# Row-wise dot products and softmax: a 64 KB row pitch in HBM for the halves, and the y loads issued by ScalarE

## The chip, the cores and the metric

The kernel runs on one core of one Trainium2 chip. The metric is device time in microseconds (us) of one launch; before the change it is 327.01 us, the median of three runs (326.87 to 327.13).

## The reference

```
gram = np.matmul(x, y.transpose(0, 2, 1))      # x, y: [8, 4096, 512] float32
diag = np.diagonal(gram, axis1=1, axis2=2)     # [8, 4096]
diag = diag - diag.max(axis=-1, keepdims=True)
exp  = np.exp(diag)
out  = exp / exp.sum(axis=-1, keepdims=True)   # [8, 4096] float32
```

Only the diagonal of the product is used, so the work is 8 x 4096 dot products of length 512, one per row, and a softmax over the 4096 results of each batch. The inputs are 64 MiB each; the output is 128 KiB.

## The kernel before

A batch has 4096 rows, which are spread over 128 partitions, 32 rows to each. The kernel handles a batch in two halves. A half is one "tile": 16 rows per partition of x in an SBUF buffer `xt` (128 partitions x 32 KB, 4 MB) and the same of y in `yt`. There are 16 tiles, numbered 0 to 15 here (batch b has tiles 2b and 2b+1); x7 is the x load of tile 7, y7 its y load. In HBM a half is one stretch of 2048 rows, and partition p takes 16 consecutive rows of it, so that a 4 MB load reads one contiguous 4 MB stretch, 32 KB after 32 KB.

Each pool of buffers has three slots (`bufs=3`). The load of tile n therefore waits until the dot products of tile n-3 are done. All loads are issued by SyncE (SP in the profile) in the order x0, y0, x1, y1 and so on (lines 43 and 44). The last tile is loaded in pieces of 8, 4, 2, 1 and 1 rows per partition, each an x and a y load; they are called a to e here (x15a is 2 MB, x15e is 256 KB). Completion is signalled over eight semaphore lanes that all DMAs use in turn, so a DMA may also wait for the completion of the DMA that had its lane before it.

VectorE (DVE) computes 16 dot products per tile and partition, one instruction for each row (line 51): it multiplies a row of `xt` with a row of `yt` and accumulates the sum into one column of `diag`. After the second half of a batch comes the softmax: a maximum over 32 columns (line 65), a maximum over the partitions on GpSimd (POOL, line 67), its negative (line 69), the exponential with a row sum on ScalarE (ACT, line 71), the sum over the partitions on GpSimd (line 76), a reciprocal and a multiplication on DVE (lines 78 and 79), and the store of the batch's results, 16 KB, issued by ACT (line 80). The store of batch b is called OUTb. Before the change it writes two runs of 64 B per partition.

Every engine executes its instructions in the order of the program as the framework has laid it out, and waits at the first one whose inputs are missing. A DMA issued by SP goes to SP's queue, one issued by ACT to ACT's queue; both queues are served by the same 16 DMA engines. A 4 MB load is 128 packets of 32 KB, 8 on each of the 16 engines.

Of the kernel before, what the change touches and what calls it, by code (L numbers as in the profile page):

```python
# [1 line left out]

# [5 lines left out]


@with_exitstack
def kernel(
    ctx: ExitStack,
    tc: tile.TileContext,
    x: bass.AP,
    y: bass.AP,
    out: bass.AP,
):
    nc = tc.nc
    f32 = mybir.dt.float32  # L20
    B, N, D = x.shape
    P = nc.NUM_PARTITIONS
    R = N // P
    H = R // 2


    xv = x.rearrange("b (h p r) d -> b h p r d", p=P, r=H)
    yv = y.rearrange("b (h p r) d -> b h p r d", p=P, r=H)
    ov = out.rearrange("b (h p r) -> b p h r", p=P, r=H)

    io = ctx.enter_context(tc.tile_pool(name="io", bufs=3))
    persist = ctx.enter_context(tc.tile_pool(name="persist", bufs=1))
    sm = ctx.enter_context(tc.tile_pool(name="sm", bufs=2))

    diag = persist.tile([P, B * R], f32, name="diag")
    res = persist.tile([P, B * R], f32, name="res")

    def load(b, r0, parts):
        xt = io.tile([P, H, D], f32, tag="xt", name="xt")
        yt = io.tile([P, H, D], f32, tag="yt", name="yt")  # L40
        o = 0
        for n in parts:
            nc.sync.dma_start(out=xt[:, o : o + n, :], in_=xv[b, r0 // H, :, o : o + n, :])  # L43
            nc.sync.dma_start(out=yt[:, o : o + n, :], in_=yv[b, r0 // H, :, o : o + n, :])
            o += n
        return xt, yt

    def dots(b, r0, xt, yt):
        for k in range(H):
            c = b * R + r0 + k  # L50
            nc.vector.scalar_tensor_tensor(  # L51
                out=xt[:, k, :],
                in0=xt[:, k, :],
                scalar=1.0,
                in1=yt[:, k, :],
                op0=mybir.AluOpType.mult,
                op1=mybir.AluOpType.mult,
                accum_out=diag[:, c : c + 1],
            )

    def softmax(b):
        db = diag[:, b * R : (b + 1) * R]
        rb = res[:, b * R : (b + 1) * R]
        mxp = sm.tile([P, 1], f32, tag="mxp", name="mxp")
        nc.vector.tensor_reduce(out=mxp, in_=db, axis=mybir.AxisListType.X, op=mybir.AluOpType.max)  # L65
        mx = sm.tile([P, 1], f32, tag="mx", name="mx")
        nc.gpsimd.partition_all_reduce(out_ap=mx, in_ap=mxp, channels=P, reduce_op=bass_isa.ReduceOp.max)  # L67
        nmx = sm.tile([P, 1], f32, tag="nmx", name="nmx")
        nc.vector.tensor_single_scalar(out=nmx, in_=mx, scalar=-1.0, op=mybir.AluOpType.mult)  # L69
        sump = sm.tile([P, 1], f32, tag="sump", name="sump")  # L70
        nc.scalar.activation(  # L71
            out=rb, in_=db, func=mybir.ActivationFunctionType.Exp,
            bias=nmx, scale=1.0, accum_out=sump,
        )
        ssum = sm.tile([P, 1], f32, tag="ssum", name="ssum")
        nc.gpsimd.partition_all_reduce(out_ap=ssum, in_ap=sump, channels=P, reduce_op=bass_isa.ReduceOp.add)  # L76
        rc = sm.tile([P, 1], f32, tag="rc", name="rc")
        nc.vector.reciprocal(out=rc, in_=ssum)  # L78
        nc.vector.tensor_single_scalar(out=rb, in_=rb, scalar=rc, op=mybir.AluOpType.mult)  # L79
        nc.scalar.dma_start(out=ov[b], in_=rb.rearrange("p (h r) -> p h r", r=H))  # L80

    for b in range(B):
        for h in range(2):
            last = b == B - 1 and h == 1
            parts = [8, 4, 2, 1, 1] if last else [H]
            xt, yt = load(b, h * H, parts)
            dots(b, h * H, xt, yt)
        softmax(b)


# [1 line left out]
_INS = ['x', 'y']  # L92
_OUTS = [((8, 4096), 'float32')]


# [23 lines left out]
```

## Time and profile before

| What | Value |
|---|---|
| median of 3 runs | 327.01 us |
| profiled execution, its own time | 327.13 us |
| its span in the profile | 325.4 us |
| DVE busy | 164.4 us (51%) |
| ACT busy, POOL busy | 4.6 us, 6.1 us |
| load queue (q1) | 5760 packets, 134.22 MB, 96.1% of 16 engines' span |
| store queue (q10) | 2176 packets, 0.13 MB, 0.5% |
| mean rate over the span | 413 GB/s |

Times within the profile are counted from the start of the span. The difference of 1.7 us between the profiled execution's time and its span lies outside the profile. A queue's share is the time that its packets took, divided by the time of 16 engines over the whole span. The landing time of a DMA counts from its issue to the signal that all of its data is there, so it contains the time that it spent behind earlier transfers of its queue.

### The profile page before, as it was taken

The page shows a single profiled execution, that of the slowest core. Times are in us where ns is not written, and L with a number is a line of the kernel's source. Part 1 is how long each engine was busy: PE and PEld are TensorE (multiplying, and loading weights), DVE is VectorE, ACT ScalarE, POOL GpSimd, SP SyncE. Part 2 cuts the span into 40 slices and gives each one's busy share as a digit, 9 for nine tenths or more (in the row PEclk, how much of TensorE's full clock was granted, in tenths as well). Part 3 has the DMA queues.
Part 4 walks back from the last instruction along what each step waited for, and adds up shares of the span by engine and source line. Part 5 has one row for each costly group of instructions (what it writes and reads, how often), then busy time and mean ns, then how long its engine had stood idle before and what let it go on. Part 6 is the DMA issues. An engine that isn't in the chain of part 4 may idle for free.

```text
span 325.4 us, 727 instructions
## 1 busy us (share of the span) xinstructions
DVE 164.4 (51%) x544; ACT 4.6 (1%) x17; POOL 6.1 (2%) x20
## 2 busy tenths in 40 slices
DVE  0029084390935619165290833909257190662992
ACT  1000000000000000000000000000000000000000
POOL 0000000000000000000000000000000000000000
DMA  8999999999999999999999999999999999999960
GB/s 322 451 411 427 451 440 403 444 452 403 435 451 424 416 451 432 407 448 448 411 431 452 409 432 447 427 415 448 436 419 435 452 405 436 447 423 414 411 250 5
DMA packets 7941, 134.39 MB, mean 413 GB/s; under 512 B 2816, under 2 KB 2816, under 8 KB 3584
## 3 DMA queue, kind: packets, MB, share of 16 engines
q1 hardware_dynamic: 5760, 134.22, 96.1%
q10 hardware_dynamic: 2176, 0.13, 0.5%
q14 instruction: 5, 0.04, 0.0%
HBM read 134.22 MB, written 0.13 MB: 413 GB/s over the span
## 4 chain that ended last, share of the span: by engine, by line
DMA 82%; DVE 16%; issue 1%; SPq 0%; POOLq 0%; POOL 0%; DVEq 0%
DMA yt<-in_y_dram 82%; DVE xt L51 15%; SPq L43 0%; DVE mxp L65 0%; POOLq L114 0%; POOL mx L67 0%; DVE res L79 0%; DVE rc L78 0%; DVEq L51 0%; DVEq L79 0%; POOLq L67 0%
## 5 line engine op out<-in xcount | busy, mean ns | idle before, releaser
L51 DVE SCALAR_TENSOR_TENSOR xt<-xt,yt 128x512 f32<-128x512 f32 x256 | 158.3, 687 | 144.2 <-DMA yt<-in_y_dram 144.2
L51 DVE DVE_READ_ACCUMULATOR xt<-xt,yt 128x1 f32 x256 | 21.1, 82 | 0.0
L67 POOL PARTITION_ALL_REDUCE mx<-mxp x8 | 2.8, 352 | 309.0 <-DVE mxp L65 309.0
L71 ACT ACTIVATE res<-diag,nmx 128x32 f32<-128x32 f32 x8 | 2.6, 321 | 315.4 <-DVE nmx L69 315.4
L78 DVE RECIPROCAL rc<-ssum 128x1 f32<-128x1 f32 x8 | 1.3, 164 | 7.7 <-POOL ssum L76 7.7
L69 DVE TENSOR_SCALAR nmx<-mx 128x1 f32<-128x1 f32 x8 | 1.2, 154 | 4.3 <-POOL mx L67 4.3
L76 POOL PARTITION_ALL_REDUCE ssum<-sump x8 | 3.1, 385 | 5.8 <-ACT res L71 5.8
L79 DVE TENSOR_SCALAR res<-res,rc 128x32 f32<-128x32 f32 x8 | 1.9, 242 | 0.9
L65 DVE TENSOR_REDUCE mxp<-diag 128x1 f32<-128x32 f32 x8 | 1.5, 186 | 0.3
L71 ACT ACTIVATION_READ_ACCUMULATOR res<-diag,nmx 128x1 f32 x8 | 1.5, 186 | 0.0
L71 ACT ACT_TABLE_LOAD x1 | 1.3, 1283 | 0.7 <-PEq L103 0.7
L103 POOL MEMSET const-float32-0.0<- 128x1 f32 x1 | 0.1, 99 | 0.2 <-issue 0.2
L103 POOL MEMSET const-bfloat16-1.0<- 128x1 bf16 x1 | 0.1, 102 | 0.0
L103 POOL MEMSET const-uint8-127<- 128x1 uint8 x1 | 0.1, 102 | 0.0
L103 POOL MEMSET const-float32-1.0<- 128x1 f32 x1 | 0.1, 99 | 0.0
## 6 DMA issues: line engine op xcount, KB each, us to landing
xt<-in_x_dram SPq DMA_DIRECT2D x15, 4096.0 KB, 39.6
yt<-in_y_dram SPq DMA_DIRECT2D x15, 4096.0 KB, 48.9
xt<-in_x_dram SPq DMA_DIRECT2D x1, 2048.0 KB, 34.8
yt<-in_y_dram SPq DMA_DIRECT2D x1, 2048.0 KB, 39.3
xt<-in_x_dram SPq DMA_DIRECT2D x1, 1024.0 KB, 35.8
yt<-in_y_dram SPq DMA_DIRECT2D x1, 1024.0 KB, 37.9
xt<-in_x_dram SPq DMA_DIRECT2D x1, 512.0 KB, 35.5
yt<-in_y_dram SPq DMA_DIRECT2D x1, 512.0 KB, 27.0
```

Source lines behind the costliest of these rows:

```text
L51: nc.vector.scalar_tensor_tensor(out=xt[:, k, :], in0=xt[:, k, :], scalar=1.0, in1=yt[:, k, :], op0=mybir.AluOpType.mult, op1=mybir.AluOpT ...
L65: nc.vector.tensor_reduce(out=mxp, in_=db, axis=mybir.AxisListType.X, op=mybir.AluOpType.max)
L67: nc.gpsimd.partition_all_reduce(out_ap=mx, in_ap=mxp, channels=P, reduce_op=bass_isa.ReduceOp.max)
L69: nc.vector.tensor_single_scalar(out=nmx, in_=mx, scalar=-1.0, op=mybir.AluOpType.mult)
L71: nc.scalar.activation(out=rb, in_=db, func=mybir.ActivationFunctionType.Exp, bias=nmx, scale=1.0, accum_out=sump,)
L76: nc.gpsimd.partition_all_reduce(out_ap=ssum, in_ap=sump, channels=P, reduce_op=bass_isa.ReduceOp.add)
L78: nc.vector.reciprocal(out=rc, in_=ssum)
L79: nc.vector.tensor_single_scalar(out=rb, in_=rb, scalar=rc, op=mybir.AluOpType.mult)
L103: nc = _bacc.Bacc("TRN2", target_bir_lowering=False, num_devices=1)
```

## The change

Three things are different. Partition p now takes 32 consecutive rows of a batch, and a half is 16 of these 32; a 4 MB load reads 128 runs of 32 KB that start 64 KB apart. The y loads are issued by ACT in place of SP. The output of a batch is one run of 128 B per partition in place of two of 64 B. Sizes of the loads, the pieces of the last tile, the number of buffers and all arithmetic stay as they are.

```diff
-    xv = x.rearrange("b (h p r) d -> b h p r d", p=P, r=H)
-    yv = y.rearrange("b (h p r) d -> b h p r d", p=P, r=H)
-    ov = out.rearrange("b (h p r) -> b p h r", p=P, r=H)
+    xv = x.rearrange("b (p r) d -> b p r d", p=P)
+    yv = y.rearrange("b (p r) d -> b p r d", p=P)
+    ov = out.rearrange("b (p r) -> b p r", p=P)
...
-            nc.sync.dma_start(out=xt[:, o : o + n, :], in_=xv[b, r0 // H, :, o : o + n, :])
-            nc.sync.dma_start(out=yt[:, o : o + n, :], in_=yv[b, r0 // H, :, o : o + n, :])
+            nc.sync.dma_start(out=xt[:, o : o + n, :], in_=xv[b, :, r0 + o : r0 + o + n, :])
+            nc.scalar.dma_start(out=yt[:, o : o + n, :], in_=yv[b, :, r0 + o : r0 + o + n, :])
...
-        nc.scalar.dma_start(out=ov[b], in_=rb.rearrange("p (h r) -> p h r", r=H))
+        nc.scalar.dma_start(out=ov[b], in_=rb)
```

The framework orders the instructions of each engine. On SP only the 20 x loads remain, each behind the release of its buffer. On ACT the order becomes y0, y1, y2, and then for each batch b: the exponential of b, y of tile 2b+3, OUTb, y of tile 2b+4. At the end it is: exponential of batch 6, y15a, OUT6, y15b, y15c, y15d, y15e, exponential of batch 7, OUT7. On DVE two rows of tile 2 now stand inside the softmax of batch 0, ahead of lines 78 and 79; the rest of its order is unchanged, and POOL's too. The lanes that gate the pieces become: x15b waits for OUT4, x15c for x13, x15d for y13, x15e for x14, y15b for y14, y15c for x15a, y15d for x15b, y15e for y15a. Before the change, by the times of SP's issues, y15c waited for x14, x15d for y14, y15d for OUT6 and y15e for y15a.

## Prediction

> **What bounds the kernel now.** I read the page's busy slices and queues first, then the chain of waits, then the instruction groups, then a table of busy time by stretches for the end, and the timeline of the last rows.
>
> ```profile
> span 325.4 us, 727 instructions
> ...
> DMA  8999999999999999999999999999999999999960
> ...
> q1 hardware_dynamic: 5760, 134.22, 96.1%
> q10 hardware_dynamic: 2176, 0.13, 0.5%
> ...
> DMA 82%; DVE 16%; issue 1%; SPq 0%; POOLq 0%; POOL 0%; DVEq 0%
> ...
> L51 DVE SCALAR_TENSOR_TENSOR xt<-xt,yt 128x512 f32<-128x512 f32 x256 | 158.3, 687 | 144.2 <-DMA yt<-in_y_dram 144.2
> ```
>
> The loads occupy all 16 engines from the first slice to the last but one; DVE works half of the time and waits 144.2 us for y. 96.1% of 325.4 us is 312.7 us of work on every DMA engine. A tile is 16 packets of 32 KB on each engine (8 of x, 8 of y); SP's issues, which follow the end of a tile's dot products, stand 19.44 us apart:
>
> ```profile
> 111.30 0.33 SPq L43 DMA_DIRECT2D xt<-in_x_dram  x1
> 111.67 0.43 SPq L44 DMA_DIRECT2D yt<-in_y_dram  x1
> 130.74 0.33 SPq L43 DMA_DIRECT2D xt<-in_x_dram  x1
> ```
>
> So a 32 KB packet takes 19.44 / 16 = 1.21 us (the trace's packet records say 1.213; 0.611, 0.309, 0.159 and 0.084 for 16, 8, 4 and 2 KB). Now the end:
>
> ```profile
> 4.00:309.00 305.00, 153.94 (x509) 2.90 (x14) 5.16 (x14) 1.00 1.00 431
> 309.00:314.00 5.00, 5.00 (x17) 0.00 (x0) 0.00 (x0) 1.00 1.02 393
> 314.00:318.00 4.00, 3.99 (x14) 0.00 (x0) 0.00 (x0) 1.00 0.08 32
> ```
>
> The column before the last is the DMA share: 1.00 until 314, then 0.08, which is one engine of 16 working 4 us longer than the others (four instruction fetches of 8 KB during the span went to it, by the packet records). And DVE, idle half of the time before, is full in these last stretches:
>
> ```profile
> 298.72 0.69 DVE L51 SCALAR_TENSOR_TENSOR xt<-xt,yt 128x512 f32<-128x512 f32 x1 [7.16 <-DMA yt<-in_y_dram]
> ...
> 318.58 0.69 DVE L51 SCALAR_TENSOR_TENSOR xt<-xt,yt 128x512 f32<-128x512 f32 x1 [0.57 <-DMA yt<-in_y_dram]
> ```
>
> From the first row of tile 14 to the last of tile 15 it waits once, 0.57 us. The reader is to see that two things limit the end together: the last bytes (318.5), and the arrival of tile 14 plus 32 rows of DVE. What delays tile 14 by more than 0.6 us delays the end, even where the last bytes come no later.
>
> **Edit 1, the addresses.** Packets keep their sizes; their starts in HBM move from 32 KB to 64 KB apart. No row shows 64 KB. The nearest: the pieces of the last tile already read 16 to 2 KB out of each 32 KB, and their packets run at 0.611 us for 16 KB, twice which is 1.222 against 1.213. Skipping addresses costs nothing there, so I take 0. A gain is excluded, since a packet of 1.213 us already differs by only 9 ns from twice the next smaller; the other end is the poorest stretch with queued loads (share 0.97, 410 GB/s in 292 to 309, against 431), +5% or 15 us.
>
> The Trainium skill, "DMA: Bandwidth & Descriptors", section "Latency and other measured facts", warns of row pitches at large powers of two; its smallest is 512 KiB, at 207 GB/s in each direction, and it falls from 2 MiB up. By it 64 KB costs nothing either, but no run here shows that page's cases.
>
> **Edit 2, the output.** OUT falls from 16 to 8 data packets per engine (2176 / 8 / 16 = 17 with the signal, then 9). At 11 ns by the packet records, seven stores beside loads save 7 x 8 x 0.011 = 0.6 us. OUT7 stays a 2.8 us landing.
>
> **Edit 3, y on ACT: issue.** Twenty issues of 0.43 us leave SP for ACT, 8.6 us on an engine busy for 4.6; covered by the y data already queued. What is new is what stands ahead: y5, for example, waits behind the exponential of batch 1, so for the dots of tile 3 and not of tile 2. These end 9.9 us after tile 3 is complete; the softmax head adds 1 us, the time from issue to first packet another 1: y5 arrives 12 us after tile 3. Its cover is y4, 8 packets, which shared with x last 19.4 us: 7 us to spare, cost 0. Where x is dry, y4 alone lasts 9.7 us and 2 us stand open, but then x's next load, released by the same dots, is due first. OUTb and y(2b+4) come with the softmax tail, 2 us later, behind y(2b+3): 0. If that cover were gone, each uncovered us would cost one only if x's queue were empty too. For OUT0 the two rows of tile 2 ahead of lines 78 and 79 mean waiting for tile 2 (near 62 us) with y3 queued: 0 as well. SP loses the in-order wait of y behind x; x is now held by its buffers alone.
>
> **Edit 3: sharing.** This is where the path moves. How two queues share an engine is shown by OUT, on ACT's queue beside the loads on SP's:
>
> ```profile
> out_dram<-res ACTq DMA_DIRECT2D x8, 16.0 KB, 22.0
> ...
> DMA to landing us min/median/max: 2.8/22.0/23.4
> ```
>
> Alone it lands in 2.8 us, beside loads in 22.0: 19.2 us for 17 packets of 11 ns. Each of them waits for about one 32 KB packet; by the packet records the 17 take 17.5 us, 0.85 turns of 1.213. So engines alternate between queues packet by packet, whatever the size. x and y alone would then advance alike, both landing when y lands now. But OUT now stands in y's queue: while its 9 packets pass, x gets 9 x 0.85 = 7.7 extra packets, nearly a whole 4 MB load (8). After OUT0, x leads by about one load, and nothing returns the lead until x's queue is empty for want of a buffer. The next OUT would make it two; three buffers don't allow more (x(n+3) waits for the dots of n), so x runs dry for a while and y takes both turns. In the middle this costs nothing: some queue always has work, total bytes stay on schedule, only tiles arrive unevenly.
>
> At the end it costs. Say the lead is one load when tile 13 is complete: x14 has landed too, x15a and x15b are in SP's queue (released by the dots of tile 12), and ACT's queue holds OUT5 and then y14. y14 needs 7.7 + 9 = 16.7 turns. In these, x passes x15a (9 turns, 8 x 0.611 = 4.9 us) and 7.7 packets of x15b (x 0.309 = 2.4 us). The engine's work up to y14 grows by L = 7.3 us. Bounds of L: 0 without any lead; all of x15, 8 x (0.611 + 0.309 + 0.159 + 2 x 0.084) = 10.0. I take 7.3, since it follows from the one-load lead, between the two.
>
> The sum: tile 14 starts at 298.7 - 0.6 + 7.3 = 305.4. Then 32 rows of 0.613 (starts 0.61 apart; 9.90 for a tile's rows in the chain) are 19.7 without a wait, since y15a to e, the only loads left for the engines, land by 318, ahead of their rows (tile 15 starts at 315.3). The last row ends at 325.1. From there to the end it was 325.4 - 319.3 = 6.1 (softmax, OUT7, closing). Span 331.2; outside it 327.13 - 325.4 = 1.7: 332.9, and 0.1 less for the median (the profiled execution was 327.13, the median is 327.01): 332.8.
>
> A rule that speaks against any effect of this edit: the same page of the Trainium skill, section "Rules for kernel authors", says that spreading DMAs over SP, ACT and GpSimd does not help, as all interleave on the same 16 engines, and saves issue time only. By it the sum would be the unchanged 327 less 0.6; by the OUT row it is 332.8.
>
> **The rivals.** (a) No lead: if y and OUT in one queue don't lose turns to x, or x is held back, tile 14 comes at 298.1 and the last bytes set the end: 327.0 - 0.6 = 326.4, between 326.0 and 327.5. For it: x's lead needs x loads queued, which the buffers limit. Against: the 22.0 us landing. (b) Faster: two queues hide the fixed 9 ns per packet. Per engine 15 x 16 + 10 x 8 = 320 packets make at most 2.9 us, and OUT 0.6: 323.5. It decides only where a 32 KB packet falls under 1.213 and there is no lead, since a lead over 3.5 us eats it. Against: engines at a share of 1.00. (c) The address pitch or the alternation of two streams costs bandwidth: at 5% some 342; it outweighs the lead once 32 KB packets take over 1.213 + 7.3 / 240 = 1.243 us. The 16 KB pieces speak against it. (d) The full lead, L = 10.0: 335.5.
>
> **How the numbers follow.** 0.2% is 0.65 us, about what a measurement tells from no change. Lead and late tile 14 (329 to 336, with (d)): 0.70. (a): 0.13, of which 0.05 falls beyond -0.65. (b): 0.07. (c): 0.10. Slower: 0.70 + 0.10 + 0.01 = 0.81; same 0.07; faster 0.12. The range leaves out (b) and most of (c): 326.4 to 336.5; the likeliest case's own is 329 to 336.
>
> **What would show it.** Packet shares near 1.00 up to 310 (edit 1 at zero); x landings far earlier than y's of the same tile after the first store; the gaps between tiles' first rows uneven, some near 10 us and others over 20, in place of 19.4; the first row of tile 14 near 305, with DVE never waiting after it; the last bytes still near 318. The prediction is wrong if x and y of a tile land together throughout, if tile 14 starts near 298, or if both queues run empty midway (the share falls under 1), which would add to it.

## The result, and the profile after

The changed kernel takes 331.92 us (median of 4 runs, 331.86 to 332.06), the kernel before 326.94 us: a ratio of 1.0154 (95% interval 1.0137 to 1.0172), 5.0 us slower. The prediction said 332.8. The profiled execution took 331.9 us with a span of 330.0.

The page of the changed kernel, with its busy slices, queues, chain and the group of the dot products:

```profile
span 330.0 us, 732 instructions
...
DVE  0029093470920561910878290660388465191995
...
DMA  8999999999999999999999999999999999999900
...
q10 hardware_dynamic: 4032, 67.24, 47.6%
q1 hardware_dynamic: 2880, 67.11, 47.5%
...
DMA 72%; DVE 24%; issue 2%; POOL 1%; ACTq 0%; POOLq 0%; DVEq 0%; ACT 0%
...
L51 DVE SCALAR_TENSOR_TENSOR xt<-xt,yt 128x512 f32<-128x512 f32 x256 | 158.1, 687 | 151.8 <-DMA yt<-in_y_dram 151.8
...
yt<-in_y_dram ACTq DMA_DIRECT2D x15, 4096.0 KB, 40.9
xt<-in_x_dram SPq DMA_DIRECT2D x15, 4096.0 KB, 29.9
```

The two queues share the engines evenly, 47.6% and 47.5%, as y and x moved the same bytes. The DMA engines are as full as before, but idle in the last two slices, where there was one such slice before. The chain has moved from DMA (82% to 72%) to DVE (16% to 24%). An x load now lands 29.9 us after its issue and a y load 40.9 us; before, it was 39.6 and 48.9.

The table of busy time by stretches (after the comma stands the busy time of DVE; the last two columns are the DMA share and GB/s):

```profile
4.00:280.00 276.00, 132.82 (x440) 2.48 (x12) 4.42 (x12) 1.00 1.00 431
280.00:300.00 20.00, 10.63 (x36) 0.41 (x2) 0.74 (x2) 1.00 1.00 427
300.00:309.00 9.00, 3.37 (x11) 0.00 (x0) 0.00 (x0) 1.00 0.98 403
309.00:314.00 5.00, 5.00 (x17) 0.00 (x0) 0.00 (x0) 1.00 1.01 397
314.00:318.00 4.00, 4.00 (x15) 0.00 (x0) 0.00 (x0) 1.00 0.09 34
318.00:322.00 4.00, 4.00 (x13) 0.00 (x0) 0.00 (x0) 1.00 0.00 0
```

The rate is 431 GB/s as before and the last bytes still move near 318. What is new is the last line: four more microseconds in which DVE is full and no data moves. The timeline of DVE follows, cut to the first rows of tiles 10 to 14 and the last row of tile 15. A line has the start, the duration, the instruction, and in brackets how long DVE stood idle before it and what ended that:

```profile
236.72 0.69 DVE L51 SCALAR_TENSOR_TENSOR xt<-xt,yt 128x512 f32<-128x512 f32 x1 [15.59 <-DMA yt<-in_y_dram]
248.95 0.69 DVE L51 SCALAR_TENSOR_TENSOR xt<-xt,yt 128x512 f32<-128x512 f32 x1 [2.34 <-DMA yt<-in_y_dram]
267.19 0.69 DVE L51 SCALAR_TENSOR_TENSOR xt<-xt,yt 128x512 f32<-128x512 f32 x1 [5.96 <-DMA yt<-in_y_dram]
287.53 0.69 DVE L51 SCALAR_TENSOR_TENSOR xt<-xt,yt 128x512 f32<-128x512 f32 x1 [10.44 <-DMA yt<-in_y_dram]
305.63 0.69 DVE L51 SCALAR_TENSOR_TENSOR xt<-xt,yt 128x512 f32<-128x512 f32 x1 [5.82 <-DMA yt<-in_y_dram]
...
324.62 0.08 DVE L51 DVE_READ_ACCUMULATOR xt<-xt,yt 128x1 f32 x1
324.62 0.69 DVE L51 SCALAR_TENSOR_TENSOR xt<-xt,yt 128x512 f32<-128x512 f32 x1
```

Tiles arrive 12.2, 18.2, 20.3 and 18.1 us apart, where they came every 19.4 to 20.4 before. Tile 14 starts at 305.63 (298.72 before), and after it DVE never waits: 31 rows later the last one starts at 324.62, against 318.58 before.

How x gets ahead can be followed in the trace's packet records (queue, start, duration and size of every packet; they name no engine, but a packet starts where the one before it on its engine ends, which puts them in order). x3 and y3 still land together, at 81.60 and 81.79 us. Then OUT0 stands in y's queue, and on each engine every one of its eight data packets follows a 32 KB packet of x: eight of them pass, which is one load. x4 lands at 91.35, y4 only at 110.94, together with x5 (110.76).

### The profile page after: what moved, and what is told of

The parts are those of the page before. It is cut to its first block, busy times and chain, and to the rows that moved or that the text cites. A ratio compares the mean times of both kernels' runs of the same rounds, so it can differ in the third digit from the quotient of the medians.

```text
span 330.0 us, 732 instructions
## 1 busy us (share of the span) xinstructions
DVE 163.9 (50%) x544; ACT 4.6 (1%) x17; POOL 6.1 (2%) x20
## 3 DMA queue, kind: packets, MB, share of 16 engines
q10 hardware_dynamic: 4032, 67.24, 47.6%
q1 hardware_dynamic: 2880, 67.11, 47.5%
## 4 chain that ended last, share of the span: by engine, by line
DMA 72%; DVE 24%; issue 2%; POOL 1%; ACTq 0%; POOLq 0%; DVEq 0%; ACT 0%
DMA yt<-in_y_dram 72%; DVE xt L51 23%; POOL mx L67 1%; DVE mxp L65 0%; DVE nmx L69 0%; ACTq L44 0%; DVE res L79 0%; POOLq L114 0%; POOL ssum L76 0%; DVE rc L78 0%; ACTq L80 0%; ACT res L71 0%; DVEq L51 0%; POOLq L67 0%; DVEq L79 0%
## 6 DMA issues: line engine op xcount, KB each, us to landing
yt<-in_y_dram ACTq DMA_DIRECT2D x15, 4096.0 KB, 40.9
xt<-in_x_dram SPq DMA_DIRECT2D x15, 4096.0 KB, 29.9
```

## The experiments

The theory: engines alternate between queues packet by packet, so a store's small packets in y's queue hand whole turns to x; x gets ahead, y14 comes late, and DVE can't make up for it. Its rivals are the new addresses, the second load queue as such, and the later issue of y.

### Undoing one part: y back on SP

```diff
-            nc.scalar.dma_start(out=yt[:, o : o + n, :], ...)
+            nc.sync.dma_start(out=yt[:, o : o + n, :], ...)
```

> The changed kernel with the y loads back on SP: new addresses and the 128 B output alone. Theory (stores on y's queue hand turns to x, tile 14 comes late): no lead, since both loads share one queue; the first row of tile 14 at 298 to 299, last bytes near 318, time 325 to 326.5. Rival (the 64 KB pitch costs rate): about as slow as the changed kernel, 331 to 332, with a 32 KB packet above 1.213 us.

Measured: 325.53 us, ratio to the kernel before 0.9961 (0.9947 to 0.9976). Two stretches of it, and in its timeline tile 14 where one queue puts it:

```profile
4.00:300.00 296.00, 145.20 (x481) 2.90 (x14) 5.17 (x14) 1.00 1.00 431
...
314.00:318.00 4.00, 3.75 (x12) 0.00 (x0) 0.00 (x0) 1.00 0.07 27
```

```profile
298.46 0.69 DVE L51 SCALAR_TENSOR_TENSOR xt<-xt,yt 128x512 f32<-128x512 f32 x1 [7.18 <-DMA yt<-in_y_dram]
...
318.34 0.69 DVE L51 SCALAR_TENSOR_TENSOR xt<-xt,yt 128x512 f32<-128x512 f32 x1 [0.58 <-DMA yt<-in_y_dram]
```

The rate is 431 GB/s as before, and by the packet records a 32 KB packet takes 1.213 us at the median, as before. So the 64 KB distance between runs costs nothing, and the change without its second queue is a gain of 1.3 us. The whole loss comes from y on ACT.

### One part alone: y on ACT with the old addresses

```diff
 (the kernel before)
-            nc.sync.dma_start(out=yt[:, o : o + n, :], ...)
+            nc.scalar.dma_start(out=yt[:, o : o + n, :], ...)
```

> The kernel before with only the y loads moved to ACT: old addresses, 64 B runs in the output, so 17 packets per engine and store. Theory: slower, tile 14 late. A store now passes 14 turns to x, nearly two loads; x then runs dry for longer and is held by its buffers, so the lead at the end is not larger than with 9 packets: first row of tile 14 at 303 to 307, time 330 to 333. Rival (the pitch): unchanged, 327. Rival (the delay grows with the number of store packets): 340.

Measured: 330.29 us, ratio 1.011 (1.0094 to 1.0125). Tile 14 again:

```profile
276.73 0.69 DVE L51 SCALAR_TENSOR_TENSOR xt<-xt,yt 128x512 f32<-128x512 f32 x1 [18.09 <-DMA yt<-in_y_dram]
288.59 0.69 DVE L51 SCALAR_TENSOR_TENSOR xt<-xt,yt 128x512 f32<-128x512 f32 x1 [1.98 <-DMA yt<-in_y_dram]
302.70 0.69 DVE L51 SCALAR_TENSOR_TENSOR xt<-xt,yt 128x512 f32<-128x512 f32 x1 [1.82 <-DMA yt<-in_y_dram]
```

The second queue alone makes the kernel slower, and the delay does not grow with the number of store packets: 17 per engine in place of 9, yet tile 14 comes at 302.70 and not later than 305.63. The cap by the three buffers shows in the packet records: x14's last packets end at 276.7 to 278.2 us, x15a is issued at 286.64, when the rows of tile 12 are done, and its first packet starts at 290.2. The packets of OUT5 run in between (284.0 to 284.8 on 15 engines, 288.1 on the last), where x has nothing to send, so they hand over no turn. What delays y14 is x15a alone: three of its packets pass on most engines, six on the engine that ends last, where y14's last packet ends at 301.53 against 297.87 with one queue (6 x 0.611 = 3.7).

### The stores in x's queue

```diff
-        nc.scalar.dma_start(out=ov[b], in_=rb)
+        nc.sync.dma_start(out=ov[b], in_=rb)
```

> The changed kernel with the stores issued by SP, in x's queue. Theory: the lead changes sides, y lands before x of the same tile after each store. But y15a is issued only after the exponential of batch 6, some 11 us after tile 13, so that near the end no y of tile 15 can take turns from x14: first row of tile 14 at 298 to 300, time 325 to 327. Rival (two load queues cost time by themselves): 331 to 332 as in the changed kernel.

Measured: 326.07 us, ratio 0.9976 (0.9967 to 0.9985). In its timeline DVE waits for another load (tiles 12 to 14):

```profile
263.50 0.69 DVE L51 SCALAR_TENSOR_TENSOR xt<-xt,yt 128x512 f32<-128x512 f32 x1 [11.78 <-DMA xt<-in_x_dram]
283.97 0.69 DVE L51 SCALAR_TENSOR_TENSOR xt<-xt,yt 128x512 f32<-128x512 f32 x1 [10.58 <-DMA xt<-in_x_dram]
298.52 0.69 DVE L51 SCALAR_TENSOR_TENSOR xt<-xt,yt 128x512 f32<-128x512 f32 x1 [2.27 <-DMA xt<-in_x_dram]
```

It is x now: the load that shares its queue with the stores is the late one. The tiles are uneven too (14.5 to 24.1 us apart from tile 3 on), but since y15a is issued only after the exponential of batch 6, nothing of tile 15 takes turns from x14 (by the packet records its eight packets on an engine have none of y between them), and tile 14 is on time. Two load queues are therefore not slow as such, and uneven tiles in the middle cost nothing here.

### No store among the loads

```diff
-        nc.scalar.dma_start(out=ov[b], in_=rb)        # in softmax(b)
...
+    nc.scalar.dma_start(                              # once, after the last softmax
+        out=out.rearrange("b (p r) -> p b r", p=P),
+        in_=res.rearrange("p (b r) -> p b r", r=R))
```

> The changed kernel with one store of all 128 KB after the last softmax in place of eight: y's queue holds loads only. Theory: x and y of each tile land together, tiles stay 19.4 to 20.4 us apart, first row of tile 14 at 297.5 to 298.5; 65 store packets per engine at the end add about 1 us: 325.5 to 327.5. Rival (two load queues, or the later issue of y behind the exponential, cost time): tile 14 near 305, time 331 to 333.

Measured: 327.27 us, ratio 1.0019 (1.0009 to 1.0029). Tile 14, and the landing time of the store:

```profile
298.32 0.69 DVE L51 SCALAR_TENSOR_TENSOR xt<-xt,yt 128x512 f32<-128x512 f32 x1 [7.19 <-DMA yt<-in_y_dram]
...
DMA to landing us min/median/max: 3.0/3.0/3.0
```

The tiles are 19.4 to 20.4 us apart all along. x on SP and y on ACT, with y behind the exponentials as in the changed kernel, keep step once no store stands between them. What it loses against one queue it loses, for the most part, after the loads: the 128 KB store lands 3.0 us after its issue, the 16 KB store of the run with one queue 1.4.

### One store, and one store fewer, ahead of y14

The next two change the stores around y14 only. The first keeps a single store in mid-stream, that of batch 5; the second takes just that one out of its place.

```diff
 (one store)
-        nc.scalar.dma_start(out=ov[b], in_=rb)
+        if b == 5:
+            nc.scalar.dma_start(out=ov[b], in_=rb)
...
+    for lo, hi in ((0, 5), (6, 8)): ...               # the others, two stores behind the last y load
 (one store fewer)
-        nc.scalar.dma_start(out=ov[b], in_=rb)
+        if b == 6:
+            nc.scalar.dma_start(out=o2, in_=...)      # batches 5 and 6 together
+        elif b != 5:
+            nc.scalar.dma_start(out=ov[b], in_=rb)
```

> The changed kernel with a single 16 KB store in mid-stream, that of batch 5 between y13 and y14; all others follow after the loads (two stores at the end). Theory: no lead until then, tiles 19.4 to 20.4 us apart; the 9 packets pass 7.7 turns, so that x14 (9 turns) and 7.7 packets of x15a (4.7 us) go ahead of y14: tile 14 at 302.5 to 303.5, time 329 to 331. Rival (a single store is hidden by the 7 us of queued y): as with one store at the end, 327.3, tile 14 at 298.3.

> The changed kernel with the store of batch 5 merged into the store of batch 6, so that no store stands between y13 and y14. Theory (a load's lead is there when tile 13 is complete, and each store packet ahead of y14 passes 0.85 turns to x15): y14 needs 9 turns in place of 16.7, x15a (4.9 us) passes it and x15b does not: first row of tile 14 at 303 (305.6 in the changed kernel), time 329 to 330. Rival (only the store in front of y14 counts, not a lead from earlier ones): tile 14 at 298.5, time 325.5.

Measured with one store: 330.96 us, ratio 1.0127 (1.011 to 1.0144). Its timeline, tiles 12 to 14:

```profile
258.87 0.69 DVE L51 SCALAR_TENSOR_TENSOR xt<-xt,yt 128x512 f32<-128x512 f32 x1 [7.17 <-DMA yt<-in_y_dram]
279.28 0.69 DVE L51 SCALAR_TENSOR_TENSOR xt<-xt,yt 128x512 f32<-128x512 f32 x1 [10.52 <-DMA yt<-in_y_dram]
303.67 0.69 DVE L51 SCALAR_TENSOR_TENSOR xt<-xt,yt 128x512 f32<-128x512 f32 x1 [12.11 <-DMA yt<-in_y_dram]
```

Everything is on time until tile 13. Then one store of 16 KB, 0.1 us of engine time, delays tile 14 by 303.67 - 298.32 = 5.35 us against the run without it. By the packet records x and y are level when y13 ends, each packet of the store stands between two packets of x, and so all eight 32 KB packets of x14 pass while the store does. y14 then takes turns with x15a, whose eight 16 KB packets all go ahead of its last one: 8 x 0.611 = 4.9 us. At 0.85 turns for a store packet, as I had it, 7.7 of them would, 4.7 us. A store packet costs a full turn here. Tile 14 fell just outside the stated 302.5 to 303.5; the last 0.4 to 0.5 of the 5.35 us arise on the engine that ends last (there y14's last packet ends at 302.89 against 297.55) and are not taken apart.

Measured with one store fewer: 329.13 us, ratio 1.0071 (1.0056 to 1.0086):

```profile
287.50 0.69 DVE L51 SCALAR_TENSOR_TENSOR xt<-xt,yt 128x512 f32<-128x512 f32 x1 [10.43 <-DMA yt<-in_y_dram]
302.79 0.69 DVE L51 SCALAR_TENSOR_TENSOR xt<-xt,yt 128x512 f32<-128x512 f32 x1 [3.01 <-DMA yt<-in_y_dram]
```

Tile 13 starts where it did in the changed kernel (287.53), tile 14 comes 2.84 us sooner. That is the part of the store of batch 5. The remaining 4.3 us (302.79 against 298.46) come from x15a, which passes y14 by the lead that earlier stores had built. By the packet records that lead is less than a load: when y13's last packet ends, two or three of x14's eight are still to go on an engine, so that five or six packets of x15a pass y14 and not eight (y14's last packet ends at 301.63 against 297.87, 3.8 us; the other 0.6 lie between it and the first row). Both halves of the working, the lead and the store in front, are thus seen apart.

### Less work for DVE at the end

Both kernels again, without the dot products of 8 rows:

```diff
-        for k in range(H):
+        for k in range(8 if b == B - 1 and r0 == H else 0, H):
...
+    nc.vector.memset(diag[:, (B - 1) * R : B * R], 0.0)
```

> The changed kernel without the dot products of the first 8 rows of tile 15 (their columns are set to 0 at the start; loads unchanged). Theory (from tile 14 on DVE sets the end): 8 x 0.613 = 4.9 us less work after tile 14, and the loads of the other pieces are there by about 318.5, so the last row ends 4 to 5 us sooner: 327 to 328.5. Rival (the last loads set the end, as before the change): within 1 us of the changed kernel, 331 to 332.

> The kernel before without the dot products of the first 8 rows of tile 15 (their columns are set to 0 at the start). Theory: the last piece still lands at 318.5, so the time stays within 0.7 us of the kernel before, 326.2 to 327.2. Rival (DVE sets the end here too): 322 to 323.

Measured: the changed kernel falls to 327.36 us, by 4.6 of the 4.9 us taken out. Its tile 14 starts where it did, and its last row 4.5 us sooner (320.09 against 324.62):

```profile
305.58 0.69 DVE L52 SCALAR_TENSOR_TENSOR xt<-xt,yt 128x512 f32<-128x512 f32 x1 [5.79 <-DMA yt<-in_y_dram]
...
320.09 0.69 DVE L52 SCALAR_TENSOR_TENSOR xt<-xt,yt 128x512 f32<-128x512 f32 x1
```

DVE sets its end. The kernel before falls to 325.73 us (ratio 0.9967, 0.9954 to 0.998), by 1.1 us, which is more than the 0.7 I had allowed. Its last row, at

```profile
318.40 0.69 DVE L52 SCALAR_TENSOR_TENSOR xt<-xt,yt 128x512 f32<-128x512 f32 x1 [0.58 <-DMA yt<-in_y_dram]
```

starts only 0.18 us sooner (318.58) and still waits for the last piece, as the theory says. The rest lies behind it: from there to the end it is 323.9 - 318.4 = 5.5 us, where the kernel before has 325.4 - 318.58 = 6.8. By the packet records, the kernel before has an instruction fetch of 8 KB at 323.18, and the last three packets of the store follow it at 323.5, while all others are done by 322.9. In this run the fetch does not occur, and the last store lands 1.6 us after its issue in place of 2.8.

### Fewer instructions on DVE

The kernel with one queue and the new addresses, with tiles 0 to 12 computed in two instructions each (the names of op and axis are shortened):

```diff
+        if b < 6 or (b == 6 and r0 == 0):
+            c = b * R + r0
+            nc.vector.tensor_tensor(out=xt, in0=xt, in1=yt, op=mult)
+            nc.vector.tensor_reduce(out=diag[:, c : c + H], in_=xt, axis=X, op=add)
+            return
```

> One load queue with the new addresses (as the run with y back on SP, 325.5 us), and tiles 0 to 12 computed with one multiplication over 8192 columns and one row-wise sum each in place of 16 instructions. Theory (the engine that works 4 us longer at the end pays about 1 us for each of four instruction fetches, which follow the count of DVE instructions): one or two fetches remain, last bytes near 315 to 316, tile 14 near 296, time 322 to 324, if the two instructions take under 19 us per tile. Rival (that engine lags for another reason, or DVE can't keep up): 325.5 or more.

Measured: 322.97 us, ratio to the kernel before 0.9887 (0.9872 to 0.9901), the quickest of all. Its groups, the stretch after 314, and the first row of tile 14 and the last of tile 15:

```profile
L51 DVE TENSOR_TENSOR xt<-xt,yt 128x8192 f32<-128x8192 f32 x13 | 113.0, 8689 | 34.1 <-DMA yt<-in_y_dram 34.1
L52 DVE TENSOR_REDUCE diag<-xt 128x16 f32<-128x8192 f32 x13 | 112.9, 8686 | 0.4
```

```profile
314.00:318.00 4.00, 2.05 (x8) 0.41 (x2) 0.57 (x2) 1.00 0.04 15
```

```profile
295.66 0.69 DVE L56 SCALAR_TENSOR_TENSOR xt<-xt,yt 128x512 f32<-128x512 f32 x1 [7.17 <-DMA yt<-in_y_dram]
...
315.62 0.69 DVE L56 SCALAR_TENSOR_TENSOR xt<-xt,yt 128x512 f32<-128x512 f32 x1 [0.57 <-DMA yt<-in_y_dram]
```

The two instructions take 8.69 us each, 17.4 per tile, under the 19.4 that a tile's data needs. The packet records show one instruction fetch among the loads in place of four, tile 14 starts at 295.66 in place of 298.46, and the lagging engine's share after 314 has shrunk from 0.07 (the run with one queue) to 0.04. The price of a fetch can be read off: it takes 0.31 to 0.33 us, and the 32 KB packet behind it 1.87 in place of 1.213 us, 0.98 us together. In the kernel before, four make 3.9, and its last bytes end at 318.04 where most engines end near 314.1; here one fetch is left, and they end at 315.07. DVE is busier (261 us in the stretches from 4 to 322, against 164), and that costs nothing.

## Why the prediction was right

**Edit 1, the addresses:** taken at 0, shown by the run with y back on SP: its 4 to 300 stretch runs at 431 GB/s as before. Rival (c) falls with it, and its second half, the alternation of two streams, by the 431 GB/s of the changed kernel from 4 to 280.

**Edit 2, the output:** 0.6 us from fewer packets was too much within the stream, where the run with one queue gains 0.26 at tile 14 (298.72 to 298.46) and 0.24 at the last row. It was missing a second part: with 128 B runs the last store no longer meets the instruction fetch. Its last packet starts at 328.82 and the fetch at 328.89 in the changed kernel, 322.53 and 322.89 with one queue. From the last row's start to the end of the span it takes 6.8 us in the kernel before, 5.4 in the changed one and 5.4 with one queue; with y on ACT and the old addresses the fetch falls on the store again (at 326.23), and it takes 6.7. That the fetch causes the longer closing is inferred from these runs. "OUT7 stays a 2.8 us landing" was wrong: it lands in 1.4. This is the term that was mis-sized: the 6.1 us from the last row's end to the end of the span measured 330.0 - 325.3 = 4.7. That is 1.4 us less, more than the 0.9 us by which the prediction was high; smaller terms went the other way (the last row 0.2 later, 0.2 more outside the span, 0.1 of the step to the median).

**The instruction fetches:** the prediction has four of them on the engine that ends late "by the packet records". The records name no engine; that all four fell on it follows from their cost, 4 x 0.98 = 3.9 us, since fetches on different engines would make none late by more than about 1 us.

**Edit 3, issue:** taken at 0. The run with one store at the end has the same y issues behind the exponentials and no late tile.

**Edit 3, sharing:** the mechanism and the place are right, and the size came out right by errors that offset each other. L was put at 7.3 us; against the run with one queue it is 305.63 - 298.46 = 7.2. Tile 14 was put at 305.4 (305.63 measured), the last row's end at 325.1 (325.3). But the assumption of a full load's lead when tile 13 is complete did not hold: x14 had not landed then. y13 lands at 287.50 and x14 at 288.73, and by the packet records two or three of x14's eight packets are still to go on an engine when y13's last one ends. Against that, a store packet passed a full turn and not 0.85. Together, all of x15a passes y14 as predicted (4.9 us), but five or six packets of x15b in place of 7.7 (1.5 to 1.9 us in place of 2.4): 6.4 to 6.8, and y14's last packet ends 6.9 us later (304.75 against 297.87). The other 0.3 us lie between that packet and the first row, a term that the prediction left out. That 7.3 stands so close to 7.2 is therefore in part luck. The run with one store fewer splits the 7.2 in another way, 4.3 by the lead and 2.8 by the store in front.

**Rivals:** (a), no lead, is what the run without stores among the loads shows, and not the changed kernel. (b), packets quickened by two queues, did not occur: 430 to 431 GB/s from 4 to 300 us with one queue and with two. (d), the full lead, did not occur either: L was 7.2 and not 10.0.

The rule of the Trainium skill that was weighed, "DMA: Bandwidth & Descriptors", section "Rules for kernel authors", holds in its wording: spreading loads over SP and ACT did not help. But it speaks of saved issue time at most, and here the spread cost 1.5%, through the order in which data arrives.

## What to carry to other kernels

A small transfer in the queue of a large one is not small: where two queues share the engines packet by packet, each of its packets gives the other queue a turn while that queue has work. Here one 16 KB store delayed the load behind it by 5.4 us in one run and 2.8 in another. Two streams that are needed in pairs were quickest in one queue (325.53 us); in two queues it depended on where the stores went (331.92 us in y's, 326.07 in x's). Uneven arrival was free while buffers covered it; look at the last tiles, where the consumer has no slack left, and ask which transfers may overtake the one that it needs.

## What the runs showed of the hardware that was not expected

- Instruction fetches share the DMA engines with the loads: with 544 DVE instructions four fetches of 8 KB fall among the loads, each costs its engine 0.98 us, and one engine finishes 4 us late; with two instructions for each of tiles 0 to 12 one fetch is left, the lag is 1 us, and the last row starts at 315.6 in place of 318.3. That the fetches are DVE's is inferred from their number following that of its instructions.
- Where the same kind of fetch falls on the last store, the closing is 1.2 to 1.4 us longer (6.8 and 6.7 us in two runs, against 5.4 to 5.5 in the others compared here).
- More store packets (17 in place of 9 per engine) did not make the kernel with two queues slower, 330.29 against 331.92 us: x had nothing to send when the store ahead of y14 passed (284.0 to 288.2 us; x15a starts at 290.2).
